# Weight splits and scaled copies tied behind the last channel tiles' gates, and a variance sum moved two portions later, in a one-core encoder kernel

## The chip, the core and the metric

The kernel runs on one core of one Trainium2 chip. The metric is the device time of one execution in microseconds (us); the median of a few executions is compared. TensorE (PE in the profile) multiplies matrices and writes PSUM, VectorE (DVE) and ScalarE (ACT) work elementwise, GpSimd (POOL) does so more slowly and cannot read PSUM, and SyncE (SP) issues transfers. Each engine takes its instructions in the order in which they were queued and waits on semaphores for the others. A difference of about 0.2% is what a measurement of this kernel can tell from no change.

## The reference, cut to what matters

One step of a small encoder runs over 640 frames (128 sample frames of 8 streams, then 512 prompt frames), 1024 channels, in float32: a convolution module, a gated feed-forward network (FFN), a chunked attention layer and a second FFN. The change touches the convolution module and the first weights of the second FFN.

```python
def conv_module(h, hist, g, w_pw1, b_pw1, w_dw, b_dw, ln_g, ln_b, w_pw2, b_pw2):
    a, gate = jnp.split(rms_norm(h, g) @ w_pw1 + b_pw1, 2, axis=-1)
    glu = a * jax.nn.sigmoid(gate)
    full = jnp.concatenate([hist.astype(glu.dtype), glu], axis=1)
    y = lax.conv_general_dilated(full, w_dw[:, None, :], (1,), "VALID", ...) + b_dw  # depthwise, width 31
    y = jax.nn.silu(layer_norm(y, ln_g, ln_b))
    return h + y @ w_pw2 + b_pw2, full[:, -CONV_HIST:]
```

## The kernel before, in words

Channels lie on the 128 partitions, so 1024 channels are 8 tiles (c = 0 to 7), and the 640 frames are two halves of 320 (g = 0, 1). A float32 product is made of three passes: each operand is split into a rounded part and a remainder (`whi`, `wlo` for weights, `xh`, `xl` for data), and `mm3` (L195) multiplies hi by hi, lo by hi and hi by lo. `wsplit` (L148) does the split of a weight tile: one transfer into `raw` (L160, from SP), one ScalarE copy to `whi` (L174, 128x2048) and one VectorE subtraction to `wlo` (L179). `raw`, `whi` and `wlo` have two buffers each. With `late=True` it only loads, and returns a function that makes the split when it is called.

The order of the work is set in two steps. The string `PLAN` (L71) says in which order the program is written: letters are steps, digits the channel tile. A planner with a simulated timeline then orders each engine's instructions by priority; `tc.high_priority` (used in `wsplit` and in the gates) moves an instruction ahead, and `tc.issue_after(ins)`, or `behind(a, b)` for several, puts every instruction of the block that runs on the same engine as `ins` behind `ins` in that engine's queue, and says nothing of the other engines. A tie on a ScalarE instruction orders ScalarE instructions alone.

The steps of the convolution module, for a channel tile c:

- The two products of the first pointwise layer and the gate are `glu_` (L748): two PSUM tiles (of four in the pool `mm`), then on ScalarE a Tanh of the second (L761, `glu_end`) and a scaled copy of the first (L764), which free the two PSUM tiles; then on VectorE the gate itself (L770 for the sample frames, L777, `gate_end`).
- The width-31 convolution is done in three ways. On TensorE (steps S, A, B; `conv_pe`, L856) go the sample frames of tile 3 and all frames of tiles 4 to 7, with small matmuls (L870) whose result a ScalarE copy (L785) takes from PSUM. They need the gated rows written to DRAM and read back shifted (`conv_shift`, L843, stores `sa`, `sb`; `conv_read`, L849, reads `xa`, `xb`, four transfers each) and a spread weight tile `w4` made by GpSimd (`conv_load`, L835, line L837). On VectorE, `conv_taps` (L802, line L816) does tiles 0 to 2 in part: one multiply-add for a tap, some held back (`HELD`) to the steps e and f. On GpSimd, `pool_taps` (L819) does the prompt frames of tile 0 and tile 3 (steps q0, q3): ScalarE makes a scaled copy `cvt` of the shifted rows for each tap (L823, four buffers), and GpSimd adds it to `ca` (L826), 31 taps in a row. `QHELD` holds the last two taps of q3 back to step e.
- Steps E6, F6, E7, F7 are the gates of the last two tiles, half by half. E7 also made `w4` for tile 7 and then read `xb` of tile 6; E6 loads and splits the weights of tile 7 and of the second pointwise layer's second pair (`pws[KT, 1]`) as soon as it can; step f splits its first pair (`pws[KT, 0]`) behind F7's gate.
- Step n (`staged_ln`, L934) does the LayerNorm statistics of half 0 between the last TensorE convolutions. Step m does the second pointwise layer for half 0 (`pw2`, L944) with the statistics of half 1 (`conv_ln`, L876) laid between its portions. `pw2` has 32 portions (four weight pairs of eight; six matmuls each). `GAPS1 = (5, 3, 10, 4)` says how many portions come before each of the four steps of `conv_ln`: the mean (L237), its spread over the partitions (L251) with subtraction, squares and the VectorE sums `acc` (L905, the last is `sum_end`), then the column sum of the squares (L237 again, then L910 and L912), then the spread of the result and the normalization (L921, L923, L186, L188). The fourth weight pair is used from portion 24 on.

The second FFN (`ffn`, L330) starts while the attention's last projection `halves` (L1365, additions L1375) runs in 16 products. Sums of squares `sqs` (L1425, L1427, the last is `sq_end`) go to a column sum on TensorE (L1434), L1436, L1438 and a spread (L1443 through L251), which the first normalized operand needs (L1444, L590). The FFN's first six weight pieces (`w_std`, L391; the splits show as L368 on ScalarE and L369 on VectorE) are tied to additions and sums by the list `lead` (L1454); the sixth was tied to `adds[11]`.

Of the kernel before, what the change touches and what calls it, by code (L numbers as in the profile page):

```python
# [15 lines left out]
P = 128  # L16
D = 1024
KT = D // P
# [8 lines left out]
W = 31  # L27
HIST = W - 1
SEG = HIST + SB
NSC = NB * SEG  # L30
# [11 lines left out]
WARM_END = 8  # L42
HP = 2000
CUT, LCUT = 8, (7, 5)
GAPS, GAPS1 = (1, 12, 2), (5, 3, 10, 4)
QHELD = 2
PO = {2: 0, 4: 1}
PL1 = (0, 2, 0, 0, 0, 0, 0, 0)
PL2 = (0, 0)
# [18 lines left out]
SSQ1 = 'aaaaaaaa'  # L68
WARM = 30, 9, 5, 5
LNO = ((0, 1, 4, 5, 6, 3, 2, 7), (0, 1, 4, 2, 3, 5, 6, 7))  # L70
PLAN = ("a0 y x1 b0 b1 q0 dp1s0 c2 k ds1p2 D3 C4 S3 q3 ds2 C5 E6 S4 A4 F6 B4 E7 e S5 A5 F7 f k k k S6 A6 "  # L71
        "S7 A7 n s0 m w1")

HELD, HELD2 = {(1, 0): 21, (2, 0): 4}, {(2, 0): 14}
# [7 lines left out]
def tile_trunk(ctx, tc, xT, vecs, hist, w_pw1, w_pw2, w_in0, w_out0, w_os0, w_in1, w_out1, w_os1,  # L82
# [744 lines left out]

    def conv_pool(c):
        acc = cp.tile([P, T], F32, tag="ca", name=nm("ca"))
        n = W - QHELD if c else W  # L830
        pool_taps(c, acc, range(n))
        return (lambda: to_y(c, NB * SB, T, acc, func=AF.Copy),
                lambda: pool_taps(c, acc, range(n, W)))

    def conv_load(c):  # L835
        w4 = w4t().rearrange("p (a b) -> p a b", a=32)
# [107 lines left out]
    def pw2(g, z):  # L944
        n = gr[g][1]
        for m2 in M2[g]:
            if (KT, m2) not in pws:
                with tc.issue_after(read_end[0]):
                    pws[KT, m2] = wsplit(w_pw2[m2], 16, P, pool=PL2[g])
            wh, wl = pws[KT, m2]  # L950
            if m2 < 2:
                del pws[KT, m2]
            pair = [mmt()[:, :n], mmt()[:, :n]]
            both = m2 == M2[0][0] and g == 0
            def part(i, ks):
                conv_end[0] = mm3(pair[i], [(wh[:, (i * 8 + k) * P:(i * 8 + k + 1) * P],
                                             wl[:, (i * 8 + k) * P:(i * 8 + k + 1) * P])
                                            for k in ks], xk(z, ks), ks[0] == 0,
                                  ks[-1] == KT - 1).ins

            if both:
                for k in range(KT):
                    part(0, range(k, k + 1))
                    part(1, range(k, k + 1))
                    yield
            else:
                for i in range(2):
                    for k in range(0, KT, 2):
                        part(i, range(k, k + 2))
                        yield  # L970
            for i in range(2):
                m = 2 * m2 + i
                pt = pair[i]
                nc.vector.scalar_tensor_tensor(out=hp(g, m), in0=pt[:, :n], scalar=col(V_BPW2, m),
                                               in1=hp(g, m), op0=ALU.add, op1=ALU.add)
# [3 lines left out]
    def step(op, arg):  # L979
        c = int(arg[-1]) if arg else 0  # L980
        if op == "a":
            glu(c, 0, *pws[c])
        elif op == "b":
            glu(c, 1, *pws[c])
        elif op == "c":
            w = pws.get(c) or wsplit(w_pw1[c], 16, P, pool=PL1[c], cuts=2)
            pws[c + 1] = wsplit(w_pw1[c + 1], 16, P)
            load_hist(c, c + 1)
            glu(c, 0, *w)
            glu(c, 1, *w)  # L990
        elif op == "y":
            load_x(1)
        elif op == "x":
            def mid():
                with behind(norm_end["xh"][2], norm_end["pow"]):
                    xs[1] = rms(1, V_NCONV, SSQ1, 8, hold=w4t)
            glu(1, 0, *pws[1], mid=mid)
        elif op in "CDEF":
            if op != "F":
                load_hist(c, c + 1)  # L1000
                w4 = conv_load(c)
                if c + 1 < KT:
                    pws[c + 1] = wsplit(w_pw1[c + 1], 16, P)
                glu_(c, 0, *pws[c], None)
                read = conv_shift(c, "a", 0, NSC if op == "D" else NXA, True)
                if c + 2 == KT:
                    pws[KT, 0] = wsplit(w_pw2[0], 16, P, late=True)
                    with tc.issue_after(store_end[0]):
                        pws[KT, 1] = wsplit(w_pw2[1], 16, P)
                x4s[c] = [w4, read(), None]  # L1010
                if c + 1 == KT:
                    with tc.issue_after(read_end[0]):
                        x4s[c - 1][2] = x4s[c - 1][2]()
                with tc.issue_after(store_end[0]):
                    nc.sync.dma_start(convs_out[:, c], gs[:, c])
            if op != "E":
                glu(c, 1, *pws[c])
                if op != "D":
                    x4s[c][2] = conv_shift(c, "b", NSC + HA, NXB, c >= KT - 2)
        elif op == "d":  # L1020
            chains, copy = conv([(int(arg[i + 1]), int(arg[i] == "p"))
                                 for i in range(0, len(arg), 2)])
            copies.append(copy)
            conv_taps(chains, HELD)
            held.extend(chains)
        elif op == "e":
            with tc.issue_after(gate_end[0]):
                conv_taps(held, HELD2)
            with tc.issue_after(glu_end[0]):
                pool_rest.pop()()  # L1030
        elif op == "f":
            with behind(gate_end[0], glu_end[0]):
                conv_taps(held, {})
                pws[KT, 0] = pws[KT, 0]()
        elif op == "k":
            with tc.issue_after(glu_end[0]):
                copies.pop(0)()
        elif op == "q":
            copy, rest = conv_pool(c)
            copies.append(copy)  # L1040
            if c == 0:
                copies.pop()()
            else:
                pool_rest.append(rest)
        elif op == "L":
            x4s[c][2] = x4s[c][2]()
        elif op in "SAB":
            for _ in conv_pe(c, op):
                pass
        elif op == "s":  # L1050
            nc.sync.dma_start(convp_out, gp[:, :, T:T + HIST])
        elif op == "n":
            staged_ln()
        elif op == "m":
            ln, products = conv_ln(1, sum_end[0]), pw2(0, zs[0])
            for gap in GAPS1:
                for _ in range(gap):
                    with tc.issue_after(conv_end[0]):
                        next(products)
                with tc.issue_after(conv_end[0]):  # L1060
                    next(ln, None)
            while next(products, 0) is None:
                pass
        elif op == "w":
            for _ in pw2(c, zs[c]):
                pass
# [378 lines left out]
    for i in range(SPREAD_AT, KT):  # L1445
        with tc.issue_after(end):
# [5 lines left out]
    hf = ExitStack()  # L1452
    spare, last_add, last_mm = ffn(1, w_in1, w_out1, w_os1, ((256, 384), (0, 256)), hf,
                                     [(split_end[0], i) for i in (adds[1], adds[3], adds[5], sq_end)] +  # L1454
                                     [(sq_end,), (adds[11],)],
                                     b0=bw)


# [126 lines left out]
```

## Time and profile before

| what | value |
| --- | --- |
| time, median of 3 executions | 1476.32 us (1474.15 to 1476.91) |
| the profiled execution's own time | 1477.64 us |
| span of the profiled execution, first to last instruction | 1475.5 us |
| mean granted TensorE clock | 0.991 |
| busy: PE, DVE, ACT, POOL | 1440.5, 1140.7, 756.6, 293.1 us |

The span is 2.1 us shorter than the execution's own time. TensorE is busy for all but 35.0 us of the span. "Busy" doesn't say how fast: the granted clock is a column of its own, and a matmul at a lower clock is counted as busy for longer. The rows of a timeline read: start in us, duration in us, engine, line, operation, output <- inputs, shapes, count; in brackets the idle time of the engine just before and what ended it. A row with a count joins neighbours, and its duration then includes the short pauses between them.

### The profile page before, as it was taken

The numbers are of one execution on the slowest core, as the hardware profiler recorded it, in microseconds if no ns is written. First come the engines' busy times: TensorE is split into PE (matmuls) and PEld (weight loads), VectorE is DVE, ScalarE is ACT, GpSimd is POOL, SyncE is SP. The second block draws the span as 40 slices with busy tenths as digits, with TensorE's granted clock in tenths as the row PEclk, the third lists the DMA queues.
The fourth block names the chain that finished last, engine by engine and source line by source line (L and its number), as shares of the span: only waits on it lengthen the run. The fifth ranks groups of instructions, "written<-read, shape, count | busy, mean of one in ns | idle before, by whom it ended". The sixth has DMA issues, their size and how long they took to land.

```text
span 1475.5 us, 28228 instructions
## 1 busy us (share of the span) xinstructions
PE 1440.5 (98%) x11030; PEld 1377.4 (93%) x11030; DVE 1140.7 (77%) x2523; ACT 756.6 (51%) x1628; POOL 293.1 (20%) x350
## 2 busy tenths in 40 slices
PE   9999999999999999999999999998999999999997
PEld 8998689999999999999988898887999999999997
DVE  6788766899789788766867768576899888788755
ACT  4666345464464464445745445443565454455443
POOL 5689002011111111013222111010001111111101
PEclk9999999999999999999999999999999999999998
DMA  7265514045444544424655554361225444544512
GB/s 241 75 180 151 152 57 143 30 113 141 134 113 120 154 108 123 136 93 154 192 186 180 189 198 162 129 208 29 80 76 142 130 120 130 135 119 118 148 60 72
DMA packets 66868, 192.56 MB, mean 131 GB/s; under 512 B 12080, under 2 KB 30256, under 8 KB 58416
## 3 DMA queue, kind: packets, MB, share of 16 engines
q1 hardware_dynamic: 52944, 161.10, 33.6%
q0 software_dynamic: 13504, 29.37, 9.8%
q8 instruction: 86, 1.41, 0.4%
q14 instruction: 46, 0.38, 0.1%
q10 hardware_dynamic: 288, 0.31, 0.1%
HBM read 179.14 MB, written 11.61 MB: 129 GB/s over the span
## 4 chain that ended last, share of the span: by engine, by line
PE 73%; DVE 10%; POOL 6%; DMA 5%; issue 3%; ACT 3%; POOLq 0%; SPq 0%; DVEq 0%; ACTq 0%
PE mm L435 41%; PE mm L198 8%; PE mm L200 7%; PE mm L199 7%; POOL ca L826 5%; DMA raw<-in_w_in 3%; DVE wlo L369 1%; DMA raw<-in_w_os 1%; PE am L1296 1%; PE w L1312 1%; PE w L237 1%; PE am L1279 1%; ACT whi L163 1%; PE am L1343 1%; DVE h L572 1%
## 5 line engine op out<-in xcount | busy, mean ns | idle before, releaser
L435 PE MATMUL mm<-XH,whi 128*128 128x320 f32 x896 | 275.6, 310 | 1.3 <-ACT t L445 0.5
L435 PE MATMUL mm<-XH,wlo 128*128 128x320 f32 x896 | 276.5, 309 | 0.0
L435 PE MATMUL mm<-XL,whi 128*128 128x320 f32 x896 | 274.5, 309 | 0.0
L368 ACT ACTIVATE whi<-raw 128x512 fp32r<-128x512 f32 (+2 forms) x280 | 169.4, 614 | 139.2 <-PE mm L435 112.8
L198 PE MATMUL mm<-xh,whi 128*128 128x320 f32 (+2 forms) x640 | 203.1, 318 | 2.9 <-ACT t L764 2.1
L199 PE MATMUL mm<-xh,wlo 128*128 128x320 f32 (+2 forms) x640 | 200.7, 314 | 0.0
L369 DVE TENSOR_TENSOR wlo<-raw,whi 128x512 fp32r<-128x512 f32 (+2 forms) x280 | 184.8, 669 | 18.4 <-ACT whi L368 16.8
L200 PE MATMUL mm<-xl,whi 128*128 128x320 f32 (+2 forms) x640 | 198.6, 314 | 0.0
L435 PE MATMUL mm<-hid,whi 128*128 128x320 f32 x732 | 171.6, 310 | 2.5 <-DVE hid L369 2.4
L435 PEld LDWEIGHTS mm<-XH,whi 128*128 128x128 f32 x896 | 167.7, 188 | 3.0 <-ACT t L445 1.7
L435 PEld LDWEIGHTS mm<-XH,wlo 128*128 128x128 f32 x896 | 168.3, 188 | 0.0
L435 PEld LDWEIGHTS mm<-XL,whi 128*128 128x128 f32 x896 | 167.7, 188 | 0.0
L435 PEld LDWEIGHTS mm<-hid,whi 128*128 128x128 f32 x732 | 124.7, 188 | 4.7 <-DVE hid L369 3.5
L198 PEld LDWEIGHTS mm<-xh,whi 128*128 128x128 f32 x640 | 122.7, 192 | 6.2 <-ACT t L764 2.5
L199 PEld LDWEIGHTS mm<-xh,wlo 128*128 128x128 f32 x640 | 122.8, 192 | 0.2
L200 PEld LDWEIGHTS mm<-xl,whi 128*128 128x128 f32 x640 | 122.0, 192 | 0.6 <-issue 0.2
L435 PE MATMUL mm<-hid,wlo 128*128 128x320 f32 x366 | 112.9, 308 | 0.0
L435 PE MATMUL mm<-XL,shi 128*128 128x320 f32 x344 | 105.4, 308 | 0.6 <-DVE XL L369 0.6
L435 PE MATMUL mm<-XH,shi 128*128 128x320 f32 x344 | 105.8, 308 | 0.0
L435 PE MATMUL mm<-XH,slo 128*128 128x320 f32 x344 | 105.7, 307 | 0.0
L414 POOL DMA_DIRECT2D s<-in_w_in x38 | 22.0, 580 | 389.2 <-DVE wlo L369 211.5
L826 POOL TENSOR_TENSOR ca<-ca,cvt 128x512 f32<-128x512 f32 x60 | 91.8, 1531 | 17.7 <-ACT cvt L823 11.1
(261 smaller groups left out, 3371.5 us busy)
## 6 DMA issues: line engine op xcount, KB each, us to landing
raw<-in_w_in SPq DMA_DIRECT2D x38, 1024.0 KB
s<-in_w_in POOLq DMA_DIRECT2D x76, 256.0 KB, 4.2
raw<-in_w_os SPq DMA_DIRECT2D x24, 768.0 KB
cache<-in_ck SPq DMA_DIRECT2D x32, 512.0 KB
cache<-in_cv SPq DMA_DIRECT2D x32, 512.0 KB
raw<-in_w_pw SPq DMA_DIRECT2D x11, 1024.0 KB
s<-in_w_os POOLq DMA_DIRECT2D x48, 192.0 KB, 3.7
raw<-in_w_kq SPq DMA_DIRECT2D x8, 1024.0 KB
```

The source lines that it names most:

```text
L163: nc.scalar.activation(out=hi[:, a:b], in_=raw[:, a:b], func=AF.Copy, scale=gain)
L198: nc.tensor.matmul(ps, wh, xh, start=(first and i == 0), stop=False)
L199: nc.tensor.matmul(ps, wl, xh, start=False, stop=False)
L200: end = nc.tensor.matmul(ps, wh, xl, start=False, stop=(stop and i == last))
L237: mean_end[0] = nc.tensor.matmul(st[:, 512 + t * w + k:513 + t * w + k], s[:, a:a + P], onec, start=True, stop=True).ins
L368: put_end[1] = nc.scalar.activation(out=hi, in_=src, func=AF.Copy).ins
L369: put_end[0] = nc.vector.tensor_tensor(out=lo, in0=src, in1=hi.bitcast(F32), op=sub).ins
L414: nc.gpsimd.dma_start(s1, src[:, 2 * n:3 * n])
L435: last = nc.tensor.matmul(pt, wt, v, start=(first and k == i == 0), stop=(k == n - 1 and i == 2), skip_group_check=True)
L572: nc.vector.tensor_tensor(out=hv, in0=hv, in1=pt, op=sub if row else add)
L826: nc.gpsimd.tensor_tensor(out=acc, in0=acc, in1=pr, op=ALU.add)
L1279: step_end[0] = nc.tensor.transpose(tr[:, o:o + P], S[:, SOFF[i] + k * P:SOFF[i] + (k + 1) * P], ident).ins
```

## The change

The prompt taps of tile 3 are cut into four runs (`POOLED = 14, 21, 29, W`): 14 at q3, 7 at a new step u behind E6's Tanh, 8 at a second u behind F6's Tanh, the last 2 at e as before. The weight split of tile 7 moves behind E6's gate and Tanh; that of the second pointwise layer's first pair from f to e (behind E7's gate and Tanh), and of its second pair from E6, untied, to f. `w4` of tile 7 is made at e, behind the last two taps in the program. `xb` of tile 6 is read as soon as it is stored, not behind tile 7's `xa`. The column sum of half 1's squares comes two portions later, and the VectorE part of the fourth pair's split goes behind the last sum of squares. In the second FFN the sixth weight piece is tied to `sq_end`.

```diff
-GAPS, GAPS1 = (1, 12, 2), (5, 3, 10, 4)
-QHELD = 2
+GAPS, GAPS1 = (1, 12, 2), (5, 3, 12, 4)
+POOLED = 14, 21, 29, W
...
-PLAN = ("... C5 E6 S4 A4 F6 B4 E7 e S5 A5 F7 f k k k S6 A6 "
+PLAN = ("... C5 E6 u S4 A4 F6 u B4 E7 e S5 A5 F7 f k k k S6 A6 "
...
     def conv_pool(c):
         acc = cp.tile([P, T], F32, tag="ca", name=nm("ca"))
-        n = W - QHELD if c else W
-        pool_taps(c, acc, range(n))
+        ends = POOLED if c else (W,)
+        pool_taps(c, acc, range(ends[0]))
         return (lambda: to_y(c, NB * SB, T, acc, func=AF.Copy),
-                lambda: pool_taps(c, acc, range(n, W)))
+                [lambda a=a, b=b: pool_taps(c, acc, range(a, b)) for a, b in zip(ends, ends[1:])])
...
-                    pws[KT, m2] = wsplit(w_pw2[m2], 16, P, pool=PL2[g])
+                    pws[KT, m2] = wsplit(w_pw2[m2], 16, P, pool=PL2[g],
+                                         ties=(sum_end[0],) if m2 == M2[0][3] and not g else ())
...
-                w4 = conv_load(c)
+                w4 = conv_load(c) if c + 1 < KT else None
                 if c + 1 < KT:
-                    pws[c + 1] = wsplit(w_pw1[c + 1], 16, P)
+                    pws[c + 1] = wsplit(w_pw1[c + 1], 16, P, late=op == "E")
                 glu_(c, 0, *pws[c], None)
+                if op == "E" and c + 1 < KT:
+                    with behind(gate_end[0], glu_end[0]):
+                        pws[c + 1] = pws[c + 1]()
...
-                        pws[KT, 1] = wsplit(w_pw2[1], 16, P)
+                        pws[KT, 1] = wsplit(w_pw2[1], 16, P, late=True)
                 x4s[c] = [w4, read(), None]
-                if c + 1 == KT:
-                    with tc.issue_after(read_end[0]):
-                        x4s[c - 1][2] = x4s[c - 1][2]()
...
-                    x4s[c][2] = conv_shift(c, "b", NSC + HA, NXB, c >= KT - 2)
+                    x4s[c][2] = conv_shift(c, "b", NSC + HA, NXB, c + 1 == KT)
...
         elif op == "e":
-            with tc.issue_after(gate_end[0]):
+            with behind(gate_end[0], glu_end[0]):
                 conv_taps(held, HELD2)
-            with tc.issue_after(glu_end[0]):
-                pool_rest.pop()()
+                pool_rest.pop(0)()
+                x4s[KT - 1][0] = conv_load(KT - 1)
+                pws[KT, 0] = pws[KT, 0]()
         elif op == "f":
             with behind(gate_end[0], glu_end[0]):
                 conv_taps(held, {})
-                pws[KT, 0] = pws[KT, 0]()
+                pws[KT, 1] = pws[KT, 1]()
+        elif op == "u":
+            with tc.issue_after(glu_end[0]):
+                pool_rest.pop(0)()
...
-                                     [(sq_end,), (adds[11],)],
+                                     [(sq_end,)] * 2,
```

More of the change, by code (lines that the diff above doesn't have):

```diff
@@ L70 @@
 LNO = ((0, 1, 4, 5, 6, 3, 2, 7), (0, 1, 4, 2, 3, 5, 6, 7))
-PLAN = ("a0 y x1 b0 b1 q0 dp1s0 c2 k ds1p2 D3 C4 S3 q3 ds2 C5 E6 S4 A4 F6 B4 E7 e S5 A5 F7 f k k k S6 A6 "
+PLAN = ("a0 y x1 b0 b1 q0 dp1s0 c2 k ds1p2 D3 C4 S3 q3 ds2 C5 E6 u S4 A4 F6 u B4 E7 e S5 A5 F7 f k k k S6 A6 "
         "S7 A7 n s0 m w1")
@@ L1042, in step @@
                 copies.pop()()
-            else:
-                pool_rest.append(rest)
+            pool_rest.extend(rest)
         elif op == "L":
```

## The prediction

> **What bounds the kernel now.** I read the busy shares first, then the table of stages around each pause of TensorE, then the timelines of the engines that end these pauses.
>
> ```profile
> PE 1440.5 (98%) x11030; PEld 1377.4 (93%) x11030; DVE 1140.7 (77%) x2523; ACT 756.6 (51%) x1628; POOL 293.1 (20%) x350
> ```
>
> TensorE bounds the kernel. Its instructions are the same before and after, so time can come from two sources: its idle 35.0 us, and stretches at a lower granted clock. In the stages that the change touches there are four pauses over a microsecond (columns: stage; its length; busy time of PE, PEld, DVE, ACT, POOL; granted clock; transfers):
>
> ```profile
> 120.30:122.41 2.11, 0.00 (x1) 0.00 (x1) 2.11 (x5) 1.14 (x2) 2.03 (x2) 1.00 0.25 68
> 122.41:126.00 3.59, 3.59 (x14) 3.59 (x15) 1.06 (x5) 2.58 (x4) 3.35 (x4) 0.52 0.53 131
> 162.10:164.10 2.00, 0.11 (x6) 0.03 (x4) 1.90 (x5) 0.28 (x1) 0.00 (x0) 1.00 0.09 6
> 203.75:207.54 3.79, 0.18 (x2) 0.00 (x1) 3.60 (x5) 0.38 (x1) 0.00 (x0) 1.00 0.28 119
> 207.54:214.93 7.39, 7.39 (x30) 7.39 (x31) 0.71 (x2) 0.00 (x0) 0.85 (x1) 0.54 0.41 142
> 1028.30:1029.92 1.62, 0.06 (x1) 0.00 (x1) 1.62 (x5) 0.00 (x0) 0.00 (x0) 1.00 0.00 0
> 1029.92:1034.00 4.08, 4.08 (x18) 4.08 (x19) 2.24 (x4) 0.00 (x0) 0.88 (x1) 0.58 0.53 146
> ```
>
> Three pauses are followed by a stretch at about half clock. At full clock that work would take 3.59 x 0.52, 7.39 x 0.54 and 4.08 x 0.58, so the stretches cost 1.72, 3.40 and 1.71 us beyond the pauses. The Trainium skill, "TensorE: Matmul & The Clock Gate", section "Why this matters for your kernels", asks for no idle gap above about 3 us; here 2.11 and 1.62 us were enough, so the trace disagrees and decides. By the page the clock terms of the first and third place would not be there to win, and the sum below would be 8.9 us instead of 12.3.
>
> **Place 1: a blocked ScalarE queue.**
>
> ```profile
> 122.41 0.53 PE L198 MATMUL mm<-xh,whi 128*128 128x320 f32 x1 [2.11 <-ACT t L764]
> 114.73 0.73 ACT L823 ACTIVATE cvt<-gall,dwv 128x512 f32<-128x512 f32 x1 [0.65 <-POOL ca L826]
> 115.77 1.90 ACT L174 ACTIVATE whi<-raw 128x2048 fp32r<-128x2048 f32 x1
> 117.57 1.32 ACT L823 ACTIVATE cvt<-gall,dwv 128x512 f32<-128x512 f32 x2
> 121.22 0.72 ACT L823 ACTIVATE cvt<-gall,dwv 128x512 f32<-128x512 f32 x1 [2.32 <-POOL ca L826]
> 121.85 0.51 ACT L764 ACTIVATE t<-mm,hb 128x320 f32<-128x320 f32 x1
> 124.56 0.51 ACT L761 ACTIVATE t<-mm,hb 128x320 f32<-128x320 f32 x1
> 127.49 0.34 ACT L785 ACTIVATE y<-mm,vec 128x128 f32<-128x128 f32 x1
> ```
>
> TensorE (first row) wants the PSUM tile of E6's first product back. The copy that frees it (L764, 121.85) stands behind a scaled copy that waits 2.32 us for a GpSimd buffer. E6's products had ended before the convolutions that begin at 115.73, so its Tanh, run at 124.56, was due at about 115.6.
>
> ```profile
> 115.73 4.57 PE L870 MATMUL mm<-xa,w 128*32 128x128 f32 x128
> 121.27 1.27 POOL ca L826
> 117.92 3.27 POOL ca L826
> 117.78 2.29 DVE L179 TENSOR_TENSOR wlo<-raw,whi 128x2048 fp32r<-128x2048 f32 x1
> 147.19 2.77 POOL L826 TENSOR_TENSOR ca<-ca,cvt 128x512 f32<-128x512 f32 x2
> 145.27 1.96 POOL L837 TENSOR_TENSOR w<-i,dwv 128x1024 f32<-128x1024 f32 x1
> ```
>
> The change ties taps 14 to 20 behind E6's Tanh. Copy 13, the last untied one, is the row at 114.73 (the copies run four ahead of GpSimd), so L764 and the Tanh come at about 115 to 116, then tile 7's split (1.90 us), then the copies. GpSimd does not run dry: its add 13, counted from tile 3's first at 98.2, is the row at 121.27 and the tied copy 14 is there by about 118.6. What stands behind the tied copies on ScalarE are S4's and A4's PSUM copies; the first was run at 127.49 before, and B4, which needs its buffer, would begin at 120.3 + 7.0 = 127.3 (F6's 48 matmuls at 0.147, place 2): perhaps 0.5 us of waiting, counted below. The second run of copies stands behind F6's Tanh at about 128, when add 17 is due too. No instruction is added; the pause and its half clock go: 2.11 + 1.72 = 3.83 us.
>
> What is late next? The tail of the step, on VectorE:
>
> ```profile
> 147.37 6.82 DVE L816 SCALAR_TENSOR_TENSOR w<-gall,dwv,w 128x128 f32<-128x128 f32 x24
> 155.31 0.49 DVE L777 SCALAR_TENSOR_TENSOR gall<-t,t 128x320 f32<-128x320 f32 x1 [1.12 <-ACT t L761]
> 157.15 2.28 DVE L179 TENSOR_TENSOR wlo<-raw,whi 128x2048 fp32r<-128x2048 f32 x1
> 166.05 0.83 PE L237 MATMUL w<-onec,acc 128*128 128x1 f32 x6 [0.16 <-DVE acc L228]
> 154.58 7.60 PE L870 MATMUL mm<-xa,w 128*32 128x128 f32 x221
> ```
>
> From F7's gate on, the chain taps, split, sums ends 0.16 us after TensorE. It keeps its length: f loses one split and gets another. It must only start 3.8 us earlier. E7's gate comes at about 139.5 (127.3, 4.5 for B4, 7.0 for E7's products, the Tanh), F7's at 155.31 - 3.83 = 151.5. In these 12.0 us VectorE has the gate (0.6), about 2 us of waiting for the moved split's `whi`, the split (2.3) and the taps (6.8): 11.7. That just fits, and I leave 0.5 us for it and for B4: **3.3 us**. Because that chain ends last, the third pause in the table, 2.00 us that no recorded wait explains, would be replaced by a wait for VectorE if it went: nothing is counted. Bounds of the place: nothing, if another ScalarE order makes TensorE wait elsewhere, and 5.8 us, with that pause gone.
>
> The moved reads of `xb` for tile 6 issue four transfers:
>
> ```profile
> 152.48 1.80 SPq L852 DMA_DIRECT2D xb<-sb  x4
> 150.64 1.74 SPq L852 DMA_DIRECT2D xa<-sa  x4
> ```
>
> They now pass in front of tile 7's `sa` store on SP. They wait for their own store and for B4 to free the buffer (127.3 + 4.5 = 131.8), so SP is held until about 133.6, and E7's gate is due at 139.5: 6 us of cover. If it failed, `xa` would be late by the 1.8 us of issue.
>
> **Place 2: the sum of squares.**
>
> ```profile
> 207.54 1.14 PE L237 MATMUL w<-onec,acc 128*128 128x1 f32 x6 [3.60 <-DVE acc L905]
> 202.68 1.68 DVE L905 TENSOR_TENSOR acc<-acc,sql 128x320 f32<-128x320 f32 x3
> 204.27 2.29 DVE L179 TENSOR_TENSOR wlo<-raw,whi 128x2048 fp32r<-128x2048 f32 x1
> 206.48 1.01 DVE L905 TENSOR_TENSOR acc<-acc,sql 128x320 f32<-128x320 f32 x2
> 219.45 1.69 DVE L188 TENSOR_TENSOR xl<-cvt,xh 128x320 fp32r<-128x320 f32 x4
> 203.33 0.31 PE L198 MATMUL mm<-xh,whi 128*128 128x320 f32 x1
> 202.89 0.31 PE L198 MATMUL mm<-xh,whi 128*128 128x320 f32 x1
> ```
>
> TensorE ran out at about 203.8; the sums ended at 207.49 because the split lay between them. The tie removes 2.29: 205.20. Two portions are 12 matmuls; three matmuls take 0.44 us (203.33 less 202.89), so 1.76 us, and TensorE arrives at 205.5. The two meet. I count 3.60 + 3.40 less 0.4 for handshakes: **6.6 us**. Behind the tied split waits L910: the split ends at about 207.5, L912 takes 0.85 (table), and the spread is due after four portions, at 209.9. The split itself is needed at portion 24, at about 210.4. The normalization keeps 8 portions, 7.0 us, of cover instead of 10; the first four `xl` pieces ended 6.2 us after the spread began (219.45 + 1.69 less 214.93). Bounds: 3.6 us, if the clock falls anyway, and 7.0.
>
> **Place 3: the second FFN's start.**
>
> ```profile
> 1029.92 0.94 PE L1434 MATMUL w<-onec,sqs 128*128 128x1 f32 x6 [1.56 <-DVE sqs L1427]
> 1027.05 1.22 DVE L369 TENSOR_TENSOR wlo<-raw,whi 128x1024 fp32r<-128x1024 f32 x1
> 1031.52 0.15 DVE L1436 TENSOR_SCALAR sqs<-w 128x3 f32<-128x3 f32 x1
> ```
>
> The piece tied to `adds[11]` ran in front of the last sums. Behind `sq_end` it costs the sums 1.22 us less, and the pause shrinks to 0.34, with 1.71 us of half clock. The moved piece may stand in front of L1436 or behind it; the spread then waits 0.4 to 1.6 us. I take 0.5, since the planner already put L1436 between waiting pieces: **2.4 us**. Bounds: 0 and 2.9.
>
> **The sum.** 3.3 + 6.6 + 2.4 = 12.3 us. Against the profiled execution's own 1477.64 us this gives 1465.3; against the median of 1476.32, 1464.0. I say 1465. After each place TensorE runs nearly without pause to the next, so a gain passes on. The bounds add to 3.6 and 15.7.
>
> **Rivals.**
>
> *The half clock stays.* The pauses shrink but the small column sums (0.83 to 1.14 us, one column each) still look idle, or the fall lands on other work. Then 6.8 us of the sum are lost: 5.5 us gained, about 1471. For it: the fall follows even 1.56 us. Against: the 2.00 us pause at 162 kept clock 1.00. The Trainium skill, the same page, section "Part 1: The HAM clock gate", says that the activity window runs freely, so that where a fall lands is chance; the trace's two unequal cases agree.
>
> *The planner only moves the waits.* A tie orders one engine: other copies may stand in front of S4's, B4's or E7's copies, and one new pause of place 1's kind at half clock (3.8 us) at two or three places takes back 8 to 12 us: 1474 to 1478. For it: the waits of ScalarE name such copies first:
>
> ```profile
> ACT cvt L823 <- POOL ca L826: 15.2, 19, 4.0
> ```
>
> These are 15.2 us in 19 waits between 96 and 145 us. Against: each new tie leaves ScalarE in front free when a gate is due.
>
> *Slower: GpSimd feeds S7 too late.* Tile 7's `w4` moves behind all taps on GpSimd. S7 is due at 154.58 + 4.4 (128 of the 221 matmuls in 7.60 us) - 3.83 = 155.15. From 122.54, 17 adds and 1.96 us must fit: 1.80 us for each add. Before, these 17 took 1.50 (up to 149.96, less 1.96), so there are 5 us to spare. Adds beside a split on VectorE take 3.27 against 1.27. Above 1.80 S7 waits 17 times the excess; above 2.7 all is lost; at 2.9 the time is about 1484. For it: copies tied behind gates can starve GpSimd, which the trace doesn't show. Against: the number of splits beside the taps doesn't grow. The Trainium skill, "SBUF — State Buffer", section "SBUF: two separate sides", says that GpSimd and a VectorE operation with two SBUF inputs exclude each other for a whole instruction; the rows at 117.78 and 117.92 agree.
>
> **Chances.** Forecast 0.60 (own range 1461 to 1469); half clock stays 0.12; waits moved, within 0.2% (about what a measurement of this kernel can tell from no change), 0.12; slower 0.16. So faster 0.72, same 0.12, slower 0.16. The range 1460 to 1479 takes in the first three.
>
> **What would show it.** Right: no pause above 0.6 us before F6's first product, granted clock 1.00 behind it; the column sum L237 after 20 portions with no wait for `acc`; no split between the sums L905 or L1427. Wrong: `cvt` copies still in front of L764 of E6; a wait of L870 for `w4` or of B4 or F7 for ScalarE; clock near 0.5 in these stages without a pause; a long wait of the spread at place 3 for L1438.

## The result, and the profile after

The changed kernel takes 1471.62 us (median of 20 executions, 1467.99 to 1474.31), the kernel before 1475.52 us in the same runs: ratio 0.9973, 95% interval [0.9966, 0.9981]. About 3.9 us are won, a third of the 12.3 us that the prediction added up: the direction was right, the size was not. The profiled execution of the changed kernel took 1471.35 us, its span 1469.5 us. The profiled execution of the kernel before, 1477.64 us, lies 2.1 us above its median, so the two profiles are 6.3 us apart where the medians are 3.9 us apart.

The busy shares of the profile after answer to the first line of the prediction:

```profile
PE 1436.2 (98%) x11030; PEld 1372.6 (93%) x11030; DVE 1138.5 (77%) x2523; ACT 758.1 (52%) x1628; POOL 293.6 (20%) x350
```

TensorE does the same 11030 matmuls and is idle for 33.3 us of the span (1469.5 less 1436.2) instead of 35.0. The stages of the table (start and end; length; busy time of PE, PEld, DVE, ACT, POOL; granted clock; transfers) show where its idle time is now:

```profile
120.44:125.00 4.56, 4.56 (x35) 4.56 (x32) 4.56 (x11) 2.87 (x6) 4.33 (x4) 1.00 0.38 90
160.03:164.06 4.03, 0.00 (x1) 0.00 (x0) 3.60 (x9) 0.59 (x2) 0.00 (x0) 0.90 0.00 0
164.06:169.51 5.45, 5.45 (x26) 4.19 (x26) 0.33 (x2) 0.00 (x0) 0.00 (x0) 0.50 0.00 0
202.00:206.09 4.09, 4.09 (x30) 3.92 (x28) 3.36 (x8) 1.92 (x1) 0.00 (x0) 1.00 0.71 256
206.09:213.00 6.91, 6.91 (x50) 6.91 (x50) 3.22 (x4) 0.00 (x0) 0.85 (x1) 1.00 0.46 152
1027.00:1028.69 1.69, 0.01 (x1) 0.00 (x0) 1.40 (x5) 0.00 (x0) 0.88 (x1) 1.00 0.84 240
1028.69:1033.00 4.31, 3.94 (x25) 3.40 (x25) 2.87 (x7) 2.23 (x5) 0.00 (x0) 1.00 0.93 321
```

The first pause at 122 is gone and so is the one at 204; behind both the clock is 1.00. In their place stands a pause of 4.03 us at 160, followed by 5.45 us at half clock, and at 1027 the pause has about the same size as before. TensorE's timeline names who ends each pause of the changed stages (start, duration, engine, line, ...; in brackets the idle time and what ended it):

```profile
164.06 1.44 PE L237 MATMUL w<-onec,acc 128*128 128x1 f32 x6 [4.03 <-DVE acc L228]
...
176.92 0.83 PE L237 MATMUL w<-onec,acc 128*128 128x1 f32 x6 [0.47 <-DVE acc L905]
...
206.09 0.83 PE L237 MATMUL w<-onec,acc 128*128 128x1 f32 x6
...
244.00 0.83 PE L251 MATMUL w<-ident,rst 128*128 128x128 f32 x6
...
248.93 0.31 PE L435 MATMUL mm<-XH,shi 128*128 128x320 f32 x1
251.17 0.42 PE L435 MATMUL mm<-XL,shi 128*128 128x320 f32 x1 [0.90 <-DVE XL L369]
...
276.10 0.42 PE L435 MATMUL mm<-XL,shi 128*128 128x320 f32 x1 [0.57 <-DVE XL L369]
...
1003.89 0.33 PE L1334 MATMUL am<-ident,Ss 128*128 128x128 f32 x1 [0.74 <-ACT PTs L1336]
...
1028.69 0.94 PE L251 MATMUL w<-ident,sqs 128*128 128x128 f32 x6 [1.68 <-POOL sqs L1442]
...
1031.31 0.41 PE L435 MATMUL mm<-XH,shi 128*128 128x320 f32 x1
```

The same instructions in the timeline of the kernel before:

```profile
176.44 0.83 PE L237 MATMUL w<-onec,acc 128*128 128x1 f32 x6 [0.74 <-DVE acc L905]
...
243.27 0.83 PE L251 MATMUL w<-ident,rst 128*128 128x128 f32 x6
...
255.24 0.31 PE L435 MATMUL mm<-XH,shi 128*128 128x320 f32 x1
...
1008.04 0.33 PE L1330 MATMUL am<-ident,Ss 128*128 128x128 f32 x1 [0.74 <-ACT PTs L1332]
...
1036.51 0.42 PE L435 MATMUL mm<-XH,shi 128*128 128x320 f32 x1
```

Set one against the other, these rows show where this pair of profiles gains and loses time. Before the statistics of half 0, the convolutions run 3.5 us earlier than before (S6 begins at 151.08 instead of 154.58), and that is place 1's gain as forecast. At 176 the changed kernel is 0.48 us *later*: all of it is lost between. At the first FFN's first product it is 6.31 us earlier, so place 2 gave 6.8 us. At 1004 it is only 4.15 us earlier: 2.2 us were lost on the way, and most of them are the pauses at 251 and 276 and one of 0.41 us at 330, none of which the kernel before has. The last pair of rows, the second FFN's first product, gives place 3: 5.20 us earlier.

### The profile page after: what moved, and what is told of

The parts are those of the page before. It is cut to its first block, busy times and chain, and to the rows that moved or that the text cites. A ratio compares the mean times of both kernels' runs of the same rounds, so it can differ in the third digit from the quotient of the medians.

```text
span 1469.5 us, 28230 instructions
## 1 busy us (share of the span) xinstructions
PE 1436.2 (98%) x11030; PEld 1372.6 (93%) x11030; DVE 1138.5 (77%) x2523; ACT 758.1 (52%) x1628; POOL 293.6 (20%) x350
## 4 chain that ended last, share of the span: by engine, by line
PE 71%; DVE 13%; POOL 5%; issue 4%; ACT 3%; DMA 3%; SPq 0%; POOLq 0%; DVEq 0%; ACTq 0%
PE mm L435 43%; PE mm L198 7%; PE mm L200 7%; PE mm L199 7%; POOL ca L826 3%; DVE w L816 2%; DVE wlo L369 1%; DMA s<-in_w_os 1%; PE am L1300 1%; PE w L1316 1%; PE am L1283 1%; ACT whi L163 1%; PE am L1347 1%; DVE wlo L179 1%; PE w L237 1%
```

## The experiments

Theory A: place 1's gain is lost on VectorE's tail, because E7's Tanh stands on ScalarE behind a tied copy, and GpSimd is late for that copy since it makes `w4` first; the split moved to f lengthens the tail. Rival B: the gain is lost to the half clock, or at another place. Theory C, formed on the way: the later column sum itself costs time at the first FFN's start. All ratios are to the kernel before, timed in the same runs.

### The three places by themselves

The first is the kernel before with the edits of place 1 alone (that is, the change without these lines):

```diff
+GAPS, GAPS1 = (1, 12, 2), (5, 3, 12, 4)
...
+                                         ties=(sum_end[0],) if m2 == M2[0][3] and not g else ())
...
+                                     [(sq_end,)] * 2,
```

> The kernel before with the convolution part alone (taps, splits, w4 and xb; place 1 of the prediction). Theory A (VectorE's tail eats it): no gain, 0 us within 1, because the 3.7 us won at F6 come back as a pause of about 4 us before the column sum L237 of half 0 and a stretch at half clock behind it. Theory B (the sum on record holds, the loss is elsewhere): 3.3 us faster, pause before that L237 under 1 us.

Measured: 1477.92 us, ratio 1.0013 [1.0000, 1.0027]. The edits with most of the diff give nothing, or lose a little. Its timeline of TensorE and VectorE:

```profile
163.88 1.44 PE L237 MATMUL w<-onec,acc 128*128 128x1 f32 x6 [4.04 <-DVE acc L228]
...
141.85 1.25 DVE L770 SCALAR_TENSOR_TENSOR gall<-t,t 128x128 f32<-128x128 f32 x1 [5.63 <-ACT t L761]
```

The pause of 4.04 us and VectorE's wait of 5.63 us for E7's Tanh are there without places 2 and 3.

The second has the two lines of place 2 alone (`GAPS1` and the tie to `sum_end`).

> The kernel before with the later column sum and the tied split of the fourth weight pair alone (place 2). Theory A: the pause of 3.6 us and its half clock go and the first FFN starts about 6.8 us earlier, but about 2 us are given back at that start, where the normalized operand comes late from VectorE: 4.6 us faster. Theory B: the gain passes on whole: 6.6 us faster.

Measured: 1471.55 us, ratio 0.9973 [0.9961, 0.9985]. Place 2 alone gives what the whole change gives. The 3.60 us in front of L237 are gone; a pause of 1.06 us for `XL` has come at the first FFN's start.

The third has the one line of place 3 alone.

> The kernel before with the sixth weight piece of the second FFN behind the last sum of squares alone (place 3). Theory A: the pause moves from the column sum (1.56 us) to the spread behind it (about 1.7 us), only the half clock goes: 1.0 us faster. Theory B: 2.4 us faster.

Measured: 1475.15 us, ratio 0.9996 [0.9987, 1.0005]: nothing that can be told from no change (the 1.0 us expected lies inside the interval). VectorE's timeline of this kernel shows why (the column sum on TensorE begins at 1025.16; L1436 needs it):

```profile
1025.63 2.35 DVE L369 TENSOR_TENSOR wlo<-raw,whi 128x1024 fp32r<-128x1024 f32 x2
...
1028.30 0.15 DVE L1436 TENSOR_SCALAR sqs<-w 128x3 f32<-128x3 f32 x1
```

Both tied pieces stand in front of L1436, 2.35 us long, so the wait moved from the column sum (1.56 us) to the spread behind it (1.68 us).

### Place 1: what makes VectorE's tail late

In the changed kernel, E7's products end at 139.36, where TensorE goes on with a convolution. The timelines of ScalarE, GpSimd and VectorE from there:

```profile
140.45 0.72 ACT L823 ACTIVATE cvt<-gall,dwv 128x512 f32<-128x512 f32 x1 [2.38 <-POOL ca L826]
...
141.49 0.52 ACT L761 ACTIVATE t<-mm,hb 128x320 f32<-128x320 f32 x1
```

```profile
137.27 1.91 POOL L837 TENSOR_TENSOR w<-i,dwv 128x1024 f32<-128x1024 f32 x1
139.15 11.61 POOL L826 TENSOR_TENSOR ca<-ca,cvt 128x512 f32<-128x512 f32 x7
```

```profile
142.04 1.25 DVE L770 SCALAR_TENSOR_TENSOR gall<-t,t 128x128 f32<-128x128 f32 x1 [5.62 <-ACT t L761]
...
145.03 3.19 DVE L179 TENSOR_TENSOR wlo<-raw,whi 128x2048 fp32r<-128x2048 f32 x1
148.15 5.27 DVE L816 SCALAR_TENSOR_TENSOR w<-gall,dwv,w 128x128 f32<-128x128 f32 x18
153.33 0.48 DVE L777 SCALAR_TENSOR_TENSOR gall<-t,t 128x320 f32<-128x320 f32 x1
...
155.16 2.28 DVE L179 TENSOR_TENSOR wlo<-raw,whi 128x2048 fp32r<-128x2048 f32 x1
```

Read from the top: a tied copy waits 2.38 us for GpSimd; the Tanh behind it comes at 141.49, 2.13 us after the products; GpSimd was late for the copy because it made `w4` (1.91 us) ahead of the last seven additions. VectorE waits 5.62 us for this Tanh, then has work without a pause up to F7's gate at 153.33, and the column sum follows 10.73 us behind that gate (10.74 before, 166.05 less 155.31). The next three experiments change one link each. The start of these stages differs by up to 1.9 us between profiles, so I compare distances inside one profile: from E7's products to its Tanh, and from S6's first matmul to the column sum (before 11.47 us, after 12.98).

The fourth kernel is the changed one with the second pair's split taken out of f and put behind the first sums of step n:

```diff
                 conv_taps(held, {})
-                pws[KT, 1] = pws[KT, 1]()
...
+            if gap == GAPS[0]:
+                with tc.issue_after(norm_end["acc"]):
+                    pws[KT, 1] = pws[KT, 1]()
```

> The changed kernel, with the split of the second pointwise layer's second pair taken out of step f and put behind the first sums of half 0 on VectorE. Theory A (VectorE's chain from F7's gate to the sums sets the pause): the pause before the column sum L237 falls from 4.0 to about 1.7 us (2.28 us less), the half clock behind it may go (2.5 us), so 2 to 5 us faster than the changed kernel, 6 to 9 us faster than before. Theory B (the pause has another cause, such as the ScalarE copies of the convolutions): the pause stays at 4 us and the time at that of the changed kernel.

Measured: 1469.56 us, ratio 0.9961 [0.9947, 0.9975]. In its TensorE timeline:

```profile
162.14 0.83 PE L237 MATMUL w<-onec,acc 128*128 128x1 f32 x6 [2.02 <-DVE acc L228]
```

The pause shrinks by 2.0 of the split's 2.28 us, and S6 to the column sum takes 10.95 us. E7's Tanh is as late as before the edit (141.63 after products that end at 139.47).

The fifth kernel is the changed one with tile 7's `w4` tied behind the last GpSimd addition of tile 3. On VectorE and ScalarE nothing changes its order.

```diff
                 pool_rest.pop(0)()
-                x4s[KT - 1][0] = conv_load(KT - 1)
+            with tc.issue_after(pool_end[0]):
+                x4s[KT - 1][0] = conv_load(KT - 1)
```

> The changed kernel, with tile 7's w4 held behind the last addition of tile 3 on GpSimd; the order on ScalarE and VectorE is unchanged. Theory A (E7's Tanh is late because ScalarE waits for a GpSimd addition that w4, 1.9 us, overtook): E7's gate comes 1.9 us earlier, F7's gate at most 1.6 us earlier (its Tanh is due at 151.7), the pause before L237 falls from 4.0 to about 2.4 us. Theory B (VectorE's own work sets F7's gate): the pause stays at 4 us.

Measured: 1469.60 us, ratio 0.9957 [0.9945, 0.9969]. Its ScalarE timeline, with E7's products ending at 137.60:

```profile
136.98 0.72 ACT L823 ACTIVATE cvt<-gall,dwv 128x512 f32<-128x512 f32 x1 [0.65 <-POOL ca L826]
...
138.02 0.52 ACT L761 ACTIVATE t<-mm,hb 128x320 f32<-128x320 f32 x1
```

The Tanh comes 0.42 us after the products instead of 2.13, the pause is 2.48 instead of 4.03 us, and S6 to the column sum takes 11.41. So `w4`'s place on GpSimd alone, through one ScalarE copy, was worth 1.6 us on TensorE.

The sixth kernel shortens the tied run instead, with `w4` left as it is, so that fewer copies are queued in front of E7's Tanh:

```diff
-POOLED = 14, 21, 29, W
+POOLED = 14, 21, 26, W
```

> The changed kernel with the runs of taps cut at 14, 21, 26 instead of 14, 21, 29: three copies fewer stand in front of E7's Tanh on ScalarE and five instead of two behind it. Theory A: E7's Tanh and gate come about 2 us earlier and the pause before L237 falls to about 2.4 us, unless GpSimd now ends so late that the last copies are missed. Theory B: the pause stays at 4 us.

Measured: 1470.50 us, ratio 0.9963 [0.9951, 0.9975]. The Tanh comes 0.11 us after the products, the split on VectorE takes 2.28 us instead of 3.19, and VectorE now waits for F7's Tanh:

```profile
141.50 2.28 DVE L179 TENSOR_TENSOR wlo<-raw,whi 128x2048 fp32r<-128x2048 f32 x1
...
150.92 0.49 DVE L777 SCALAR_TENSOR_TENSOR gall<-t,t 128x320 f32<-128x320 f32 x1 [1.95 <-ACT t L761]
```

The split is shorter because it starts first. One addition on GpSimd, of the changed kernel and then of this one, shows it:

```profile
144.78 1.30 POOL L826 TENSOR_TENSOR ca<-ca,cvt 128x512 f32<-128x512 f32 x1
...
141.72 3.21 POOL L826 TENSOR_TENSOR ca<-ca,cvt 128x512 f32<-128x512 f32 x1 [0.55 <-ACT cvt L823]
```

In the changed kernel the addition is under way when the split starts at 145.03; here it starts 0.22 us after the split, and it is the addition that takes longer.

Yet S6 to the column sum takes 11.41 us again, with a pause of 2.47. That is the floor that the tail in f sets: F7's gate follows 0.67 us behind S6's start, and the column sum 10.74 us behind the gate. No earlier Tanh of E7 can do better; only a shorter tail can. The times of the fourth, fifth and sixth kernels can't be told from that of the changed kernel, since their intervals overlap with 0.9966 to 0.9981; what these three show, they show by the distances in their timelines.

### Place 3: one piece further back

The seventh kernel ties the sixth piece behind L1440 (the former L1436).

```diff
-                                     [(sq_end,)] * 2,
+                                     [(sq_end,), (eps_end,)],
```

> The changed kernel with the sixth weight piece of the second FFN tied behind the small VectorE operation L1440 instead of behind the last sum of squares. Theory A (two pieces of 1.2 us stand in front of L1440): the pause of 1.68 us before the spread L251 falls by 1.2 us, and the time by as much. Theory B (the chain column sum, L1440, GpSimd power takes that long anyway): the pause stays.

Measured: 1471.53 us, ratio 0.9969 [0.9960, 0.9979]. The spread's pause is 1.39 instead of 1.68 us: 0.3 us less, where I had expected 1.2. The column sum begins on TensorE at 1023.81, and one piece (1024.28, 1.22 us) still stands in front of L1440, which ends at 1025.96. That is 2.15 us after the column sum instead of 3.29, so 1.1 us are won there. The next two rows of this kernel, and the same power on GpSimd in the changed kernel, show where most of it went:

```profile
1025.88 1.21 DVE L369 TENSOR_TENSOR wlo<-raw,whi 128x1024 fp32r<-128x1024 f32 x1
1026.11 1.73 POOL L1442 TENSOR_TENSOR sqs<-sqs,mhalf 128x3 f32<-128x3 f32 x1 [9.87 <-DVE sqs L1440]
...
1027.75 0.88 POOL L1442 TENSOR_TENSOR sqs<-sqs,mhalf 128x3 f32<-128x3 f32 x1 [10.92 <-DVE sqs L1440]
```

The moved piece now runs beside the power that the spread waits for, and the power takes 1.73 us instead of 0.88. Neither theory had this.

### The pieces together

The eighth kernel has the edits of the fourth, fifth and seventh.

> The changed kernel with three edits together: the second pair's split behind the first sums (as in e4), w4 behind the last addition (as in e5), and the sixth piece behind L1440 (as in e7). Theory A: the pause before L237 goes to about 0.5 us with the clock at 1.00 behind it, and the spread's pause to 0.5 us: 8 to 11 us faster than the kernel before. Theory B: no more than e4, about 6 us faster than before.

Measured: 1467.37 us, ratio 0.9942 [0.9929, 0.9954]: 8.5 us faster than before and faster than the changed kernel. Its TensorE timeline:

```profile
159.15 0.83 PE L237 MATMUL w<-onec,acc 128*128 128x1 f32 x6
...
244.75 0.41 PE L435 MATMUL mm<-XL,shi 128*128 128x320 f32 x1 [0.90 <-DVE XL L369]
```

In front of the first row there is no wait at all, and S6 to the column sum takes 9.35 us: with both links undone, place 1's gain passes on. The pause at the first FFN's start stays, 0.90 us as in the changed kernel. The spread's pause is 1.39 us as in the seventh kernel, not the 0.5 us that I expected, and the power takes 1.73 us here too.

### Place 2: its two halves, and the first FFN's start

The ninth kernel is the kernel before with the tie of the fourth pair's split alone; the tenth has the later column sum alone, `GAPS1 = (5, 3, 12, 4)`.

> The kernel before with one half of place 2 alone: the fourth pair's VectorE split tied behind the last sum of squares, the column sum still after 18 portions. If the prediction's working of place 2 holds, the sums end 2.29 us earlier, at about 205.2, while TensorE still runs out at about 203.8: the pause in front of L237 shrinks from 3.60 to about 1.3 us, and the time falls by 2.3 us or, if the clock stays up behind the shorter pause, by up to 5.7: ratio 0.996 to 0.9985. Rival: the split is late for portion 24 when it stands behind the sums; then a pause of up to 2 us comes at about 210 and the ratio is 0.999 to 1.001.

> The kernel before with the other half of place 2 alone: the column sum two portions later, the split untied. If the prediction's working holds, TensorE arrives 1.76 us later and the sums end at about 207.5 as before, so 1.6 to 2.0 us of the pause stay: ratio 0.9965 to 0.999. Rival: with the later due time the planner puts the split behind the sums by itself, the pause goes altogether and this half alone gives what both give (0.9973).

Measured: the tie alone 1471.94 us, ratio 0.9970 [0.9958, 0.9981]; the later column sum alone 1475.53 us, ratio 0.9995 [0.9984, 1.0006]. TensorE's timelines, of the tie alone first:

```profile
205.80 0.83 PE L237 MATMUL w<-onec,acc 128*128 128x1 f32 x6 [1.67 <-DVE acc L905]
...
240.20 0.83 PE L251 MATMUL w<-ident,rst 128*128 128x128 f32 x6
250.47 0.41 PE L435 MATMUL mm<-XH,shi 128*128 128x320 f32 x1
251.75 0.31 PE L435 MATMUL mm<-XL,shi 128*128 128x320 f32 x1
```

and of the later column sum alone:

```profile
205.98 1.45 PE L237 MATMUL w<-onec,acc 128*128 128x1 f32 x6 [2.18 <-DVE acc L905]
...
246.37 0.83 PE L251 MATMUL w<-ident,rst 128*128 128x128 f32 x6
251.88 0.31 PE L435 MATMUL mm<-XH,shi 128*128 128x320 f32 x1
254.15 0.41 PE L435 MATMUL mm<-XL,shi 128*128 128x320 f32 x1 [0.93 <-DVE XL L369]
```

As worked out, each half takes its part from the pause of 3.60 us (1.93 and 1.42 us). In the time the tie alone gives what was expected, and the later column sum alone does not: 0.9965 to 0.999 was expected. But the tie alone has no pause at the first FFN's start, though TensorE is early there, and the later column sum alone has one, though TensorE arrives there later than with the tie alone. What differs is the place that the planner gives to the FFN's spread, L251: 12.0 us ahead of the first product in the kernel before, 10.3 with the tie alone, 5.5 with the later column sum alone, 4.9 in the changed kernel. In the changed kernel the chain from this spread to the first `XL` takes 7.1 us (spread 0.8, a copy, eight products L590 at 3.79 us in all, two additions and L419 at 1.6, `XL` 0.5), and TensorE wants `XL` about 6.3 us behind the spread: 0.9 us short, as the row shows.

The eleventh kernel is the eighth with L419 tied behind the last `XL` of that operand in the first FFN.

```diff
-            with tc.high_priority(offset=HP), behind(*ties()):
+            with tc.high_priority(offset=HP), behind(*ties(), *x11_end):
```

> The version of the eighth run with one more tie, in the first FFN alone: the VectorE sums of the first seven-product weight (L419, 0.68 us) go behind the last XL remainder of the first normalized operand. Theory (the first FFN's start is now set by VectorE: spread, eight L590, additions, L419, XL): the pause in front of the first XL product shrinks from 0.90 to about 0.25 us, the two later pauses (0.57, 0.55) stay; 0.6 us, ratio 0.9935 to 0.9942. Rival: the XL pieces wait for ScalarE's XH copies or the additions of half 1, or the planner rearranges what is in front of them: the pause stays at 0.9 and nothing is won.

Measured: 1466.34 us, ratio 0.9932 [0.9920, 0.9945]. In TensorE's timeline:

```profile
247.42 0.42 PE L435 MATMUL mm<-XL,shi 128*128 128x320 f32 x1 [0.30 <-DVE XL L369]
```

The pause is 0.30 us: VectorE's order in front of `XL` sets it. The time is not to be told from the eighth kernel's.

The twelfth kernel is the eighth with the column sum after 21 portions, `GAPS1 = (5, 3, 11, 4)`.

> The version of the eighth run with the column sum of half 1's squares after 21 portions instead of 22 (GAPS1 = (5, 3, 11, 4)). Theory (the later column sum moves the first FFN's spread, L251, from 10 to 12 us down to 4.9 us ahead of its first product, and this brings the pauses of 0.9 and 0.6 us there): with one portion the pause in front of the half's column sum is 0.8 us (half of 1.67), and if the FFN's spread keeps its place of 10 us, the pauses at the FFN's start go: ratio 0.993 to 0.9945, about equal to the eighth run or a little below it. If the spread comes at 4.9 us again, both prices are paid and the ratio is 0.995. Rival (the FFN's pauses come from TensorE's earlier arrival alone): the spread's place makes no difference, and pauses of 0.9 and 0.6 us stay wherever it stands.

Measured: 1466.95 us, ratio 0.9932 [0.9918, 0.9945]. The pauses are those of the middle: 0.79 us in front of the column sum, and 0.73 us in front of `XL`, with the spread 5.5 us ahead of the first product. Both prices are paid, and the sum is about that of the eighth kernel (where I had said 0.995 for this case). The eighth, eleventh and twelfth can't be told apart.

## Why the prediction was right or wrong

**Place 1, counted at 3.3 us, gave nothing.** The step that removes the blocked queue was right: the pause at 122 went with its half clock, and S6 begins 3.5 us earlier. The step that failed is "E7's gate comes at about 139.5 (127.3, 4.5 for B4, 7.0 for E7's products, the Tanh)". It came at 142.04, since the Tanh did not follow the products. The prediction took for granted that "Tile 7's `w4` moves behind all taps on GpSimd". The tie that puts it there is on ScalarE's Tanh and orders ScalarE alone; on GpSimd the planner put `w4` ahead of seven additions, and the last copy of the second run waited for them. The fifth kernel shows this link, worth 1.6 us. What I feared of GpSimd, being late for S7, did not come; it was late for a copy that a gate stood behind. The rival "The planner only moves the waits" named just this, copies in front of E7's, and I gave it 0.12; at place 1 it is what happened.

The remark "That just fits" was right in itself: from E7's gate to F7's gate VectorE took 11.3 us of the 12.0 allowed, and "It keeps its length" held to 0.01 us. The dearer step is "nothing is counted" for the third pause. The pause that no recorded wait explained, 1.89 us before, is absent after, and TensorE arrived at 160.03 to meet a tail that was only 2.0 us earlier than before, at 164.06. So 4.03 us of pause replaced it, and behind it the stretch of small column sums took 5.45 us at clock 0.50 (the table above). In the kernel before, the same stretch reads:

```profile
166.05:169.02 2.97, 2.97 (x26) 2.31 (x26) 0.33 (x2) 0.30 (x1) 0.00 (x0) 1.00 0.00 0
```

Together: 2.0 won by the tail, 2.5 lost to the clock, 0.48 us later than before. The prediction saw that a wait for VectorE could take the place of this pause, and put the exchange at nothing, though it had just counted 1.7 to 3.4 us of half clock behind each of three other waits. Rival B is thus half right, but the tail comes first: where it is shortened, in the eighth kernel, the pause and the fall of the clock are both gone. (The eleventh, with 0.41 us of pause left there, still has a low stretch of 3.4 us; the twelfth, also with 0.41 us, has none.)

**Place 2, counted at 6.6 us, gave 6.8 at its own place in the profile** and, alone, about 4.0 in the time (ratio 0.9973). The working of each half holds within half a microsecond (2.29 and 1.76 counted, 1.93 and 1.42 measured; both fall short by about the 0.4 that the prediction took off for handshakes), and the split itself, at 205.95 behind the last sum, made nothing late. The step that failed is "After each place TensorE runs nearly without pause to the next, so a gain passes on". The later column sum takes the first FFN's spread nearer to its products, and some 2 us are lost there. The two portions were not worth their price: the tie alone gives as much as both.

**Place 3, counted at 2.4 us,** is the mis-sized term: 1.05 us in the profile of the changed kernel (its first product of that FFN 5.20 us earlier, where 4.15 had arrived), and none in the time that could be told, alone. The step "the spread then waits 0.4 to 1.6 us. I take 0.5, since the planner already put L1436 between waiting pieces" took the wrong end. Two pieces of 2.35 us stood in front, and the spread waited 1.68. Among its signs of being wrong the prediction had named just this wait.

**The half clock** was counted at 1.72 + 3.40 + 1.71 us, as if each fall belonged to its pause. In one execution it doesn't: with the very pause of place 1 left in (2.09 us), the second kernel's profile has clock 1.00 between 120 and 140, and with 3.60 us left in at place 2 the third kernel's has 0.91 between 200 and 220 where the kernel before has 0.83. So these terms were sizes of one execution. What they come to on average can be estimated, since the mean granted clock of every execution is on record: (1 - clock) x span is the time lost to the clock, and the rest is about what the time would be at full clock. (Every profile also has a low stretch at its very end, which is in the first column of all.) Means, with the standard error behind:

| kernel | executions | lost to the clock, us | the rest, us |
| --- | --- | --- | --- |
| before (timed with the next three) | 30 | 10.4 (0.5) | 1465.8 (0.2) |
| place 1 alone | 11 | 13.8 (0.5) | 1464.1 (0.3) |
| place 2 alone | 12 | 6.4 (0.7) | 1465.4 (0.3) |
| place 3 alone | 11 | 9.0 (0.4) | 1465.9 (0.2) |
| changed | 20 | 8.0 (0.5) | 1463.5 (0.3) |

Part of a low stretch can fall on a pause, where it costs nothing (0.8 us of it in the changed kernel, in front of 164.06), so the split between the columns is good to about a microsecond. By this estimate the clock terms of places 2 and 3 did come on average, 4.0 and 1.4 us. That of place 1 came with the wrong sign: 3.4 us more are lost, since the new pause of 4 us brings a fall of its own. In all the clock gave 2.4 us of the 6.8 counted. The pauses gave 2.3 us of the 5.5 counted, and most of what is missing there is place 2's: 0.4 us, where 3.2 were counted.

The time, 1471.62 us, is outside the forecast's own range of 1461 to 1469 and on the number of the rival "The half clock stays", about 1471. Half of that rival happened, as a fall landed on other work; but it needed a new pause, and the falls at places 2 and 3 went. That the numbers meet is luck. In the rival on GpSimd one sum is off: 17 additions lose 12.3 us when each takes 0.72 us more, which is 2.5 us, not 2.7.

**The unexplained pause near 162** comes in the kernel before (1.89 us) and in the four kernels without the edits of place 1 (1.44 to 1.85), and in none of the nine that have them. The traces point to a cause that the prediction did not look for. The list of DMA queues has one for instructions, `q8`, that brings 86 blocks of 16 KB; that is one for about 256 of TensorE's 11030 matmuls and as many weight loads, and the blocks do come that far apart. In the five kernels with the pause, and in no other, the block due in these convolutions comes only 487 to 517 instructions after the last, and TensorE goes on 1.4 to 1.7 us after it has landed (in the kernel before it landed at 162.50, and TensorE went on at 164.07). Until then the reads of `xb` and `xa` keep the DMA engines full (share 1.07 from 154 to 162). The change reads `xb` of tile 6 some 12 us earlier; the share from 154 to 160 is 0.24, and the blocks come on time, at 153.78 and 158.56. No run moves these reads alone, so this stays a reading of the traces. Not settled either: that the first FFN's spread moves with the column sum is shown by the ninth and tenth kernels, but why the planner puts it there was not tried.

## What to carry to other kernels

A tie orders one engine, so for each tied instruction ask what the planner may now put ahead of it on the engines that feed it: here a weight tile on GpSimd, bound by no tie, delayed a copy, and the copy a Tanh. When a pause is removed, work out when every engine's chain reaches the next meeting point, not TensorE's alone; the gain ends where the first chain that didn't move comes in. And price a half clock by the mean clock of many executions, not by the one in the profile; then ask whether the new order brings a pause that has a fall of its own.

## What the runs showed of the hardware

The granted clock after a pause is not a function of its length. Five kernels keep a pause of about 2.1 us near 121: three go on at 0.50 (2.11, 2.14 and 2.13 us, in the kernel before, the ninth and the tenth), two at 1.00 (2.09 and 2.12 us, in the second and the third). 1.67 us was followed by 1.00 in the ninth, and 2.18 us by 0.50 in the tenth. The Trainium skill, "TensorE: Matmul & The Clock Gate", section "Part 1: The HAM clock gate", has the activity window run freely, and these pairs fit it: the same pause can fall into one window or across two. Between 100 and 1100 us the low stretches of all the profiles last 3.4 or 6.8 us, so each costs about 1.7 or 3.4 us, as in the prediction's table.

The clock also fell with no pause at all. In the fifth, sixth and eleventh kernels TensorE works without a break through 24 matmuls of one column (the column sums of half 1, about 2.8 us) and is at half clock behind them or from among them. In the sixth:

```profile
187.70:192.00 4.30, 4.30 (x18) 4.30 (x19) 0.34 (x2) 0.00 (x0) 0.00 (x0) 0.50 0.00 0
```

In the other kernels the clock stayed at 1.00 behind the same sums. Whether such sums count as idle for the clock, as the rival "The half clock stays" supposed, no run here tests.

A VectorE split of 128x2048 and an addition on GpSimd did not run side by side. The split took 2.28 us where it started first (the sixth kernel, 141.50), and there the addition took 3.21 us against 1.30. In the changed kernel an addition was under way at the start of a split twice: with 0.32 us still to run the split took 2.47 us (124.81), with 1.05 us to run 3.19 us (145.03). The Trainium skill, "SBUF — State Buffer", section "SBUF: two separate sides", has the two exclude each other for a whole instruction, and these rows agree: whichever starts second waits for the rest of the other. The power on GpSimd in the seventh kernel, 1.73 us beside a split instead of 0.88, fits this too.
